# A float32 trunk of two macaron layers on one core: a plain first part of four feature tiles instead of five, and the low parts of the normalized features and of their sums computed by GpSimd instead of VectorE

## The chip, the cores and the metric

One core of one Trainium2 chip runs the whole program in one launch. The metric is the device time of one execution in microseconds (us), the median of three runs. Engines carry the names of the profile: PE is TensorE (PEld its weight loads), DVE is VectorE, ACT is ScalarE, POOL is GpSimd, SP is SyncE, which issues the weight transfers.

## What is computed

Input x is 512 positions by 1024 features, float32, one batch. Two layers run one after the other, each in three steps:

```python
def swiglu(h, w_gate, w_up, w_down):
    return (jax.nn.silu(h @ w_gate) * (h @ w_up)) @ w_down
...
        x = x + 0.5 * swiglu(rms_norm(x, ffn1_norm[l]), ffn1_w_gate[l], ffn1_w_up[l], ffn1_w_down[l])
        h = rms_norm(x, mix_norm[l])
...
        x = x + jnp.concatenate([conv_out, diff_out], axis=-1) @ w_out[l]
        x = x + 0.5 * swiglu(rms_norm(x, ffn2_norm[l]), ffn2_w_gate[l], ffn2_w_up[l], ffn2_w_down[l])
```

The gate and up matrices are 1024 by 2816, the down matrix 2816 by 1024. The middle step (a causal convolution group beside a differential attention group) is the same in both kernels and is called the mixer below. The change lies in the four SwiGLU blocks, called FFN 1 to 4 in the order in which they run.

## The kernel before

**Data and products.** x stays in SBUF with features on the partitions: eight tiles of 128 features by 512 positions. Each float32 number of a product is split in two: a high part rounded to the fp32r type (a copy on ACT) and a low part, the number minus its high part (a subtract, on DVE for most). A product is three fp32r matmuls that add up in PSUM: high by high, high by low, low by high. Lines 136 to 142 (`mm3`) issue these for matmuls of 512 columns, lines 374 to 380 (`product`) for those of 256. The normalized x of the plain part lacks its row factor r; its parts are `acth` and `actl`, and r is multiplied in as the result leaves PSUM (L710, L712).

**One FFN** (`ffn`, L682 to L752) works through the 22 feature tiles of 128 hidden features in the three parts of `PARTS` (L45).

*The plain part* takes the first five tiles. A tile is 48 matmuls of 512 columns for gate and up. Then come silu on ACT (L711), the product on DVE (L713), and the split of that product (`Gated.plain`: `hh` by ACT at L624, `hl` by DVE at L625). Once all tiles are through, the plain down products run, three matmuls per tile for each of the eight output tiles, with weights brought together by `gather` (L121) in chunks of eight 128-column blocks and split at L101 and L102. Each output tile's PSUM is added to x at L730.

*The two other parts* take eight and nine tiles with a scheme of seven half-size products in place of eight (a Winograd form of the 2 by 2 block product). A unit of class `GateUp` does one tile with 84 matmuls of 256 columns, a unit `Down` two of eight output tiles. Each unit needs sums of its weight blocks, made by POOL (L355 to L358), and four split operands named A, B, C and D (ACT at L364, DVE at L368). The units follow each other; a unit issues the parts of the next one at fixed places between its own products (`body`).

**The operands of the feature side** for these units are made in `Halves`, during the plain part. Eight times L310 forms hn, a tile of x times gain times r. For each of four steps j, DVE makes three sums of halves of two tiles (L314 to L317, four operations of 256 columns, `ht` with two slots that the steps take in turn), ACT takes their high parts (L318, `th`, 768 columns), and L319 their low parts (`tl`). Before the plain down products, `settle` overwrites `acth` and `actl` with the high and low parts of the eight hn themselves (L324 and L325): the gate and up products of the plain part, which read the old content, must have ended for that. Unit 0 of the first of the two parts reads `th`, `tl`, `acth` and `actl`.

**What sets the order.** The program is written as above, and a scheduler with a timeline of its own fixes the order of instructions on each engine when the kernel is built; `keep_in_program_order` pins some of them. On the chip each engine runs its queue strictly in that order and waits on semaphores. Rings of buffers bound how far loads run ahead: five raw weight blocks (`wraw`), four high parts, four low parts; a raw block comes free once its low part has been computed. In the first FFN only, `aside` (L687) puts some preparation of the attention bias into the loop over plain tiles.

Of the kernel before, what the change touches and what calls it, by code (L numbers as in the profile page):

```python
# [15 lines left out]
ALU = mybir.AluOpType  # L16
# [25 lines left out]
HS = SEQ // 2  # L42


PARTS = ((0, 5, 0), (5, 8, 3), (13, 9, 3))  # L45
PLAIN = PARTS[0][1]
PIN = False

# [20 lines left out]
def trunk(ctx: ExitStack, tc: tile.TileContext, xt, par, lamv, relb, onehot,  # L69
          gu1, dn1, wag, wqkv, wout, gu2, dn2, out):  # L70
    nc = tc.nc
    V, S, G, T = nc.vector, nc.scalar, nc.gpsimd, nc.tensor
# [9 lines left out]
    def f32(ap):  # L82
        return ap.bitcast(F32)
# [22 lines left out]
    def chunk(src, eng=None, pin=False):  # L106
        raw, hi, lo = ring("wraw"), ring("whi"), ring("wlo")
        nc.sync.dma_start(raw, src)
        parts_of(raw, hi, lo, eng, pin=pin)
        return hi, lo  # L110
# [36 lines left out]
    acth = act.tile([P, KT, SEQ], F32R, tag="acth", name="acth")  # L147
    actl = act.tile([P, KT, SEQ], F32R, tag="actl", name="actl")
# [17 lines left out]
    for k0, k1 in ((0, 1), (1, 4), (4, KT)):  # L166
        h = slice(k0 * P, k1 * P)
# [14 lines left out]
    def col(l, name, i=0):  # L182
        c = _AT[name] + i
        return pars[l][:, c : c + 1]
# [31 lines left out]
    class Prep:  # L216


        def __init__(self, l, gain):
            self.l, self.gain = l, gain  # L220
            self.hi, self.lo = acth, actl
            self.s = tmp.tile([P, SEQ], F32, tag="ssum", name="ssum", bufs=1)
# [35 lines left out]
    def lead_products(pr, w, ps):  # L258

        for k in range(KT):  # L260
            for n in range(2):
                for i in range(2):
                    mm3(ps[n][i], wpart(w[n][i], k), pr[k], k == 0, k == KT - 1)

        for k in range(KT):
            pr.squares(k, pin=True)

    def first_products(pr, w, ps, early=False):


        if not early:
            rc, v = rows_rstd(pr.s, DM)
            r = spread(rc, "rb")
        for k in range(KT):
            if early and k == STATS_AT:
                rc, v = rows_rstd(pr.s, DM, pin=True)
            for i in range(2):
                mm3(ps[0][i], wpart(w[0][i], k), pr[k], k == 0, k == KT - 1, pin=early and k in (0, STATS_AT))
        for i in range(2):
            for k in range(KT):  # L280
                if early and i == 0 and k == STATS_AT:
                    r = spread(rc, "rb", pin=True)
                mm3(ps[1][i], wpart(w[1][i], k), pr[k], k == 0, k == KT - 1, pin=early and k in (0, STATS_AT))
        return rc, v, r
# [4 lines left out]
    def pair_banks(turn):  # L289
        tag = turn_tag(turn)  # L290
        return [bank(tag, "ps_pair") for _ in range(2)]


    class Halves:
# [4 lines left out]
        def __init__(self, fp, pr, r):  # L299
            self.th = fp.tile([P, 3, KT // 2, HS], F32R, tag="th", name="th")  # L300
            self.tl = fp.tile([P, 3, KT // 2, HS], F32R, tag="tl", name="tl")

            self.whole = []
            free = [f"{t}{n}" for t in ("hh", "hl") for n in range(5, 9)]
            a, b = slice(0, HS), slice(HS, SEQ)
            ht = fp.tile([P, 2, 3, HS], F32, tag="ht", name="ht")
            for j in range(KT // 2):
                for k in (j, j + KT // 2):
                    h = fp.tile([P, SEQ], F32, tag=free.pop(), name="hn")
                    V.scalar_tensor_tensor(h, x[:, k, :], col(pr.l, pr.gain, k), r, op0=ALU.mult, op1=ALU.mult)  # L310
                    self.whole.append((k, h))
                (_, ha), (_, hb) = self.whole[-2:]
                t = ht[:, j % 2]
                V.tensor_tensor(t[:, 1], hb[:, b], ha[:, b], op=ALU.subtract)  # L314
                V.tensor_tensor(ha[:, b], ha[:, a], ha[:, b], op=ALU.subtract)
                V.scalar_tensor_tensor(t[:, 0], ha[:, b], -1.0, hb[:, b], op0=ALU.mult, op1=ALU.subtract)
                V.scalar_tensor_tensor(t[:, 2], t[:, 0], -1.0, hb[:, a], op0=ALU.mult, op1=ALU.subtract)  # L317
                S.activation(self.th[:, :, j, :], t, AF.Copy)  # L318
                V.tensor_tensor(self.tl[:, :, j, :], t, f32(self.th[:, :, j, :]), op=ALU.subtract)  # L319

        def settle(self):

            for k, h in self.whole:
                S.activation(acth[:, k, :], h, AF.Copy)  # L324
                V.tensor_tensor(actl[:, k, :], h, f32(acth[:, k, :]), op=ALU.subtract)  # L325

        def get(self, name):
            if name[0] == "t" and name != "t1":
# [353 lines left out]
    def ffn(pr, gu, dn, after, turn, lead=None, aside=None):  # L682
        with tc.tile_pool(name="ffn", bufs=1) as fp:
            r = halves = None
            held, h = [], Gated(fp, 0)
            for m in range(PLAIN):
                if m == 4 and aside:  # L687
                    aside()
                if lead and m < 2:
                    w = lead[m]  # L690
                else:
                    w = [(by_halves if lead and m == 2 else chunk)(gu[m, 0]), chunk(gu[m, 1])]
                held.append((m, w, pair_banks(turn + m)))
                if m == 0:
                    continue
                if m == 1 and lead:
                    lead_products(pr, [h[1] for h in held], [h[2] for h in held])
                    continue
                if m == 1:
                    _, _, r = first_products(pr, [h[1] for h in held], [h[2] for h in held])  # L700
                elif r is None:
                    rc = products(pr, w, held[-1][2][0], 0, 4, lambda: rows_rstd(pr.s, DM, pin=True)[0])
                    r = products(pr, w, held[-1][2][1], 1, 3, lambda: spread(rc, "rb", pin=True))
                else:
                    for i in range(2):
                        products(pr, w, held[-1][2][i], i)
                for n, _, ps in held:
                    gs = fp.tile([P, 2, SEQ], F32, tag="gn", name="gs", bufs=2)
                    us = gs[:, 1]
                    V.tensor_tensor(gs[:, 0], ps[0], r, op=ALU.mult)  # L710
                    S.activation(gs[:, 0], gs[:, 0], AF.Silu)  # L711
                    V.tensor_tensor(us, ps[1], r, op=ALU.mult)  # L712
                    V.tensor_tensor(us, us, gs[:, 0], op=ALU.mult)  # L713
                    h.plain(n, us)
                held = []
                if not halves:
                    halves = Halves(fp, pr, r)
            turn += PLAIN
            halves.settle()
            blocks = [divmod(kk, HALF) for kk in range(PLAIN)]  # L720
            blocks = [(half, m * HALF + f) for m in range(KT) for half, f in blocks]
            w = None
            for m in range(KT):
                ps = bank(turn_tag(turn + m // 2), "ps_d")
                for kk in range(PLAIN):
                    b = m * PLAIN + kk
                    if b % 8 == 0:
                        w = gather(dn, blocks[b : b + 8])
                    mm3(ps, wpart(w, b % 8), h.hh[kk], kk == 0, kk == PLAIN - 1)
                V.scalar_tensor_tensor(x[:, m, :], ps, 0.5, x[:, m, :], op0=ALU.mult, op1=ALU.add)  # L730
            turn += KT // 2

            units = []
            for m0, many, pairs in PARTS[1:]:
                h = Gated(fp, pairs)
                for n in range(many):
                    units.append(GateUp(fp, turn, halves, gu[m0 + n, 0], gu[m0 + n, 1], n, h))
                    turn += 1
                end = m0 + many == FT
                for q in range(KT // 2):  # L740
                    units.append(Down(fp, turn, dn, m0, many, pairs, q, h, after if end else lambda m: None,
                                      end and q == KT // 2 - 1))
                    turn += 1
            units[0].load()
            for k in "ABDC":
                units[0].hi(k, False)
                units[0].lo(k, False)
            for n, unit in enumerate(units):
                unit.body(units[n + 1] if n + 1 < len(units) else None, units[n - 1] if n else None,
                          units[n - 2] if n > 1 else None)  # L750
            units[-1].rest()
        return turn  # L752
# [371 lines left out]
    def aside():  # L1124
        make_scalars()
        make_bias()
# [92 lines left out]
```

## Time and profile before

| | |
|---|---|
| median of three runs | 1775.17 us (1774.72 to 1776.59) |
| the profiled execution | 1774.2 us, of which the span in the trace is 1772.4 us |
| granted clock of TensorE | 1.00 |
| first matmul of the units, FFN 1 to 4 | 89.9, 627.5, 970.2, 1507.9 us |

The profiled execution is one run, and all rows of a trace belong to it. A row of a timeline has the start and the duration in us, the engine, the line, the operation, out<-in with the shapes, the count (x3: three back to back), and in brackets the idle time before it with what ended that. Groups of a line have busy time in us, the mean duration in ns, and idle time. Matmuls are pipelined: a row's duration is longer than the distance to the next, and the distance of the starts is what one costs.

### The profile page before, as it was taken

The page shows a single profiled execution, that of the slowest core. Times are in us where ns is not written, and L with a number is a line of the kernel's source. Part 1 is how long each engine was busy: PE and PEld are TensorE (multiplying, and loading weights), DVE is VectorE, ACT ScalarE, POOL GpSimd, SP SyncE. Part 2 cuts the span into 40 slices and gives each one's busy share as a digit, 9 for nine tenths or more (in the row PEclk, how much of TensorE's full clock was granted, in tenths as well). Part 3 has the DMA queues.
Part 4 walks back from the last instruction along what each step waited for, and adds up shares of the span by engine and source line. Part 5 has one row for each costly group of instructions (what it writes and reads, how often), then busy time and mean ns, then how long its engine had stood idle before and what let it go on. Part 6 is the DMA issues. An engine that isn't in the chain of part 4 may idle for free.

```text
span 1772.4 us, 30241 instructions
## 1 busy us (share of the span) xinstructions
PE 1762.0 (99%) x11725; PEld 1617.0 (91%) x11725; DVE 1395.4 (79%) x1997; ACT 985.2 (56%) x1579; POOL 965.3 (54%) x665
## 2 busy tenths in 40 slices
PE   9999999999999999999999999999999999999999
PEld 7899999988788899999988999999887888999998
DVE  6978787868857878788767887877788588787875
ACT  6456465645845456466534664665558354564653
POOL 2276566379863156566304655653798533565661
PEclk9999999999999999999999999999999999999999
DMA  6232333422122233333332333334230232223332
GB/s 225 98 111 96 107 108 105 142 88 95 37 84 85 82 98 110 104 105 116 114 96 72 108 97 108 106 99 152 72 117 27 72 108 75 105 96 108 108 105 75
DMA packets 74225, 177.87 MB, mean 100 GB/s; under 512 B 8951, under 2 KB 30726, under 8 KB 74080
## 3 DMA queue, kind: packets, MB, share of 16 engines
q1 hardware_dynamic: 72480, 174.10, 29.6%
q8 instruction: 92, 1.51, 0.3%
q0 software_dynamic: 1312, 1.67, 0.3%
q14 instruction: 53, 0.43, 0.1%
q10 hardware_dynamic: 288, 0.16, 0.0%
HBM read 173.79 MB, written 3.42 MB: 100 GB/s over the span
## 4 chain that ended last, share of the span: by engine, by line
PE 89%; DVE 6%; issue 2%; POOL 2%; ACT 1%; DMA 0%; DVEq 0%; SPq 0%; ACTq 0%
PE ps_pair L378 48%; PE ps_pair L142 5%; PE ps_pair L141 5%; PE ps_pair L138 5%; PE ps_d L378 3%; DVE wlo L368 2%; PE ps_d L141 2%; PE ps_d L138 2%; PE ps_d L142 2%; PE ps_sc L990 2%; PE ps_pair L868 2%; PE ps_pair L867 2%; PE ps_pair L866 2%; PE ps_out L142 1%; PE ps_out L141 1%
## 5 line engine op out<-in xcount | busy, mean ns | idle before, releaser
L368 DVE TENSOR_TENSOR wlo<-wraw,whi 128x1024 fp32r<-128x1024 f32 (+4 forms) x400 | 507.0, 1269 | 171.4 <-ACT whi L364 170.5
L364 ACT ACTIVATE whi<-wraw 128x1024 fp32r<-128x1024 f32 (+4 forms) x400 | 373.5, 935 | 331.5 <-PE ps_pair L378 151.7
L355 POOL TENSOR_TENSOR wraw<-wraw 128x512 f32<-128x512 f32 (+1 forms) x100 | 127.8, 1278 | 554.7 <-DVE wlo L368 376.5
L378 PE MATMUL ps_pair<-actl,whi 128*128 128x256 f32 x1088 | 307.9, 283 | 0.0
L378 PE MATMUL ps_pair<-acth,wlo 128*128 128x256 f32 x1088 | 307.9, 283 | 0.0
L378 PE MATMUL ps_pair<-acth,whi 128*128 128x256 f32 x1088 | 307.9, 283 | 0.0
L378 PE MATMUL ps_pair<-th,whi 128*128 128x256 f32 x816 | 231.7, 284 | 0.9
L378 PE MATMUL ps_pair<-tl,whi 128*128 128x256 f32 x816 | 230.9, 283 | 0.0
L378 PE MATMUL ps_pair<-th,wlo 128*128 128x256 f32 x816 | 230.9, 283 | 0.0
L101 ACT ACTIVATE whi<-wraw 128x1024 fp32r<-128x1024 f32 (+3 forms) x124 | 123.4, 1001 | 155.4 <-PE ps_pair L141 83.1
L378 PEld LDWEIGHTS ps_pair<-acth,whi 128*128 128x128 f32 x1088 | 208.9, 192 | 0.2
L378 PEld LDWEIGHTS ps_pair<-actl,whi 128*128 128x128 f32 x1088 | 208.9, 192 | 0.2
L378 PEld LDWEIGHTS ps_pair<-acth,wlo 128*128 128x128 f32 x1088 | 208.9, 192 | 0.0
L141 PE MATMUL ps_pair<-actl,whi 128*128 128x512 f32 x448 | 174.5, 391 | 0.3
L142 PE MATMUL ps_pair<-acth,wlo 128*128 128x512 f32 x448 | 173.9, 390 | 0.0
L138 PE MATMUL ps_pair<-acth,whi 128*128 128x512 f32 x448 | 173.1, 392 | 0.2
L357 POOL TENSOR_TENSOR wraw<-wraw 128x512 f32<-128x512 f32 (+1 forms) x100 | 168.1, 1681 | 7.8
L358 POOL TENSOR_TENSOR wraw<-wraw 128x512 f32<-128x512 f32 (+1 forms) x100 | 163.6, 1636 | 7.8
L378 PEld LDWEIGHTS ps_pair<-th,whi 128*128 128x128 f32 x816 | 156.6, 192 | 2.5 <-ACT keep L427 2.5
L378 PEld LDWEIGHTS ps_pair<-tl,whi 128*128 128x128 f32 x816 | 156.6, 192 | 0.0
L378 PEld LDWEIGHTS ps_pair<-th,wlo 128*128 128x128 f32 x816 | 156.6, 192 | 0.0
L356 POOL TENSOR_TENSOR wraw<-wraw 128x512 f32<-128x512 f32 (+1 forms) x100 | 151.0, 1510 | 7.6
(203 smaller groups left out, 4404.7 us busy)
## 6 DMA issues: line engine op xcount, KB each, us to landing
wraw<-in_gu SPq DMA_DIRECT2D x172, 512.0 KB, 3.4
wraw<-in_wqkv SPq DMA_DIRECT2D x24, 512.0 KB, 3.5
wraw<-in_wag SPq DMA_DIRECT2D x16, 512.0 KB, 3.4
wraw<-in_wout SPq DMA_DIRECT2D x16, 512.0 KB, 3.5
wraw<-in_dn SPq DMA_DIRECT2D x60, 128.0 KB, 3.0
wraw<-in_dn SPq DMA_DIRECT2D x20, 384.0 KB, 3.1
wraw<-in_dn SPq DMA_DIRECT2D x28, 256.0 KB, 2.9
wraw<-in_dn SPq DMA_DIRECT2D x20, 320.0 KB, 3.4
```

What stands on the lines that cost most here:

```text
L101: S.activation(hi, raw, AF.Copy)
L138: first = T.matmul(ps, wh, xh, start=start, stop=False)
L141: T.matmul(ps, wh, xl, start=False, stop=False)
L142: T.matmul(ps, wl, xh, start=False, stop=stop)
L355: G.tensor_tensor(d, g1, u1, op=ALU.add)
L356: G.tensor_tensor(u1, u1, u2, op=ALU.add)
L357: G.tensor_tensor(m0, u1, g1, op=ALU.add)
L358: G.tensor_tensor(m1, m0, g2, op=ALU.add)
L364: pinned(S.activation(hi[:, : self.cols[k]], self.raw[k][:, : self.cols[k]], AF.Copy), pin)
L368: pinned(V.tensor_tensor(out=lo[:, :c], in0=self.raw[k][:, :c], in1=f32(hi[:, :c]), op=ALU.subtract), pin)
L378: mm = T.matmul(ps, l, r, start=first and i == n == 0, stop=False, skip_group_check=True)
L866: T.matmul(ps[n], xh[:, t], wh, start=k == 0, stop=False)
```

## The change

Five lines change. The plain part takes four tiles, the second part nine; the third stays. The low parts `tl` (four of 768 columns in each FFN) and `actl` (eight of 512 in each FFN) are subtracted by POOL. `aside` is called one tile earlier in the loop, at the last tile of four as before at the last of five.

```diff
-PARTS = ((0, 5, 0), (5, 8, 3), (13, 9, 3))
+PARTS = ((0, 4, 0), (4, 9, 3), (13, 9, 3))
...
                 S.activation(self.th[:, :, j, :], t, AF.Copy)
-                V.tensor_tensor(self.tl[:, :, j, :], t, f32(self.th[:, :, j, :]), op=ALU.subtract)
+                G.tensor_tensor(self.tl[:, :, j, :], t, f32(self.th[:, :, j, :]), op=ALU.subtract)
...
                 S.activation(acth[:, k, :], h, AF.Copy)
-                V.tensor_tensor(actl[:, k, :], h, f32(acth[:, k, :]), op=ALU.subtract)
+                G.tensor_tensor(actl[:, k, :], h, f32(acth[:, k, :]), op=ALU.subtract)
...
             for m in range(PLAIN):
-                if m == 4 and aside:
+                if m == 3 and aside:
                     aside()
```

The scheduler builds the order anew. In the built kernel the mixers and the third parts have the same orders as before on DVE, ACT, POOL and SP; the plain part and the second part of each FFN differ.

## The prediction

> **What bounds the kernel now.** I read the page's busy line, its chain of waits, then the timelines of PE, DVE and POOL around the second of the four FFN calls, which the change rebuilds.
>
> ```profile
> span 1772.4 us, 30241 instructions
> PE 1762.0 (99%) x11725; PEld 1617.0 (91%) x11725; DVE 1395.4 (79%) x1997; ACT 985.2 (56%) x1579; POOL 965.3 (54%) x665
> PE 89%; DVE 6%; issue 2%; POOL 2%; ACT 1%; DMA 0%; DVEq 0%; SPq 0%; ACTq 0%
> 90.02 25.81 PE ps_pair L378 x215
> ```
>
> PE works 99% of the span, so only two things move the time: the number of matmuls, and stops that are put into PE's stream. The last line is a piece of the chain: 215 matmuls of 256 columns in 25.81 us, 0.120 us each. Those of 512 columns follow each other at 0.227 us, as the end of the plain gate and up products of FFN 2 shows:
>
> ```profile
> 600.09 0.39 PE L142 MATMUL ps_pair<-acth,wlo 128*128 128x512 f32 x1
> 600.32 0.39 PE L138 MATMUL ps_d<-hh,whi 128*128 128x512 f32 x1
> ...
> 627.29 0.39 PE L142 MATMUL ps_d<-hh,wlo 128*128 128x512 f32 x1
> 627.52 0.28 PE L378 MATMUL ps_pair<-acth,whi 128*128 128x256 f32 x1
> ```
>
> The plain down products follow without a stop, and unit 0 follows them. The stage holds together because DVE is just in time: a row further down shows the last tile's low part (L625) at 609.86, ending at 610.55, and the down products that need it come after 48 others, at 600.32 + 48 x 0.227 = 611.2. The slack is 0.7 us. That is the place where the change acts.
>
> Whether DVE is in time depends on POOL. These are the rows of POOL and of DVE in the same stretch:
>
> ```profile
> 595.71 1.30 POOL L355 TENSOR_TENSOR wraw<-wraw 128x512 f32<-128x512 f32 x1 [35.71 <-DMA wraw<-in_gu]
> 597.09 2.17 POOL L356 TENSOR_TENSOR wraw<-wraw 128x512 f32<-128x512 f32 x1
> 599.34 1.63 POOL L357 TENSOR_TENSOR wraw<-wraw 128x512 f32<-128x512 f32 x1
> 601.04 1.63 POOL L358 TENSOR_TENSOR wraw<-wraw 128x512 f32<-128x512 f32 x1
> ```
>
> ```profile
> 575.91 1.21 DVE L102 TENSOR_TENSOR wlo<-wraw,whi 128x1024 fp32r<-128x1024 f32 x1
> 577.04 0.67 DVE L625 TENSOR_TENSOR hl<-gs,hh 128x512 fp32r<-128x512 f32 x1
> 577.64 0.41 DVE L315 TENSOR_TENSOR hn<-hn 128x256 f32<-128x256 f32 x1
> 577.98 0.41 DVE L316 SCALAR_TENSOR_TENSOR ht<-hn 128x256 f32<-128x256 f32 x1
> ...
> 594.46 0.95 DVE L319 TENSOR_TENSOR tl<-ht,th 128x768 fp32r<-128x768 f32 x1
> 595.33 0.68 DVE L710 TENSOR_TENSOR gs<-ps_pair,rb 128x512 f32<-128x512 f32 x1
> 595.94 2.15 DVE L102 TENSOR_TENSOR wlo<-wraw,whi 128x1024 fp32r<-128x1024 f32 x1
> 598.02 3.50 DVE L325 TENSOR_TENSOR actl<-hn,acth 128x512 fp32r<-128x512 f32 x2
> 601.44 1.78 DVE L368 TENSOR_TENSOR wlo<-wraw,whi 128x512 fp32r<-128x512 f32 x1
> ...
> 607.88 0.68 DVE L325 TENSOR_TENSOR actl<-hn,acth 128x512 fp32r<-128x512 f32 x1
> 608.49 0.68 DVE L713 TENSOR_TENSOR gs<-gs 128x512 f32<-128x512 f32 x1
> 609.86 0.69 DVE L625 TENSOR_TENSOR hl<-gs,hh 128x512 fp32r<-128x512 f32 x1 [0.70 <-ACT hh L624]
> ```
>
> Alone, a DVE subtract of 1024 columns takes 1.21 us, of 512 0.68, and they start 1.14 and 0.60 apart (0.34 for 256 columns). While POOL adds, the same L102 takes 2.15 and two L325 take 3.50. POOL's adds stretch too, from 1.30 to 2.17 and 1.63. So a DVE operation with two operands in SBUF and a POOL operation do not run side by side here: they take turns, one by one. From 595.94 to 603.22 DVE did work of 1.14 + 2 x 0.60 + 0.60 = 2.94 us and POOL the rest of L355 and three adds of 1.3, 4.97 us: 7.9 us of work in 7.28 us. I use that factor, 0.92, for work of both in one row.
>
> **The change part by part.** *Matmuls.* Per FFN the plain part loses one tile: 48 matmuls of gate and up and 24 of down, of 512 columns. The second part gains one unit, 84 of 256 columns, and its four Downs, now nine tiles wide, gain 6 of 512 each. Net: -48 x 0.227 + 84 x 0.120 = -10.9 + 10.1 = -0.8 us, four times: **-3.2 us**. This holds only while PE doesn't wait. The added unit brings what each unit of the third part brings already, whose nine units and nine-wide Downs run in before without a stop; I cost its sums, low parts and loads at nothing, hidden by its 84 matmuls (10.1 us).
>
> *DVE to POOL.* Per FFN eight low parts of 512 columns (L325) and four of 768 (L319) leave DVE:
>
> ```profile
> L325 DVE TENSOR_TENSOR actl<-hn,acth 128x512 fp32r<-128x512 f32 x32 | 29.1, 937 | 0.0
> L319 DVE TENSOR_TENSOR tl<-ht,th 128x768 fp32r<-128x768 f32 x16 | 14.9, 948 | 0.0
> L975 POOL TENSOR_TENSOR actl<-u,acth 128x512 fp32r<-128x512 f32 x6 | 6.6, 1094 | 1.7 <-ACT acth L974 1.7
> L102 POOL TENSOR_TENSOR wlo<-wraw,whi 128x1024 fp32r<-128x1024 f32 x44 | 105.4, 2401 | 31.6 <-ACT whi L101 31.6
> ```
>
> POOL's own rows for such a subtract are 1.094 us at 512 columns and 2.401 at 1024, so about 1.75 at 768 (my estimate between the two). DVE is freed of 8 x 0.60 + 4 x 0.87 = 8.3 us, POOL is given 8 x 1.09 + 4 x 1.75 = 15.7 us. On two engines that don't run side by side the stage's joint work grows by 7.4 us, while one tile fewer makes the stage 16 us shorter.
>
> *Order and waits.* The built order decides the rest. In FFN 2 and 4, POOL's queue is: sums L355 and L356 of unit 0, a low part L319, L357, L319, L358, then all eight L325 and the last two L319. The buffer ht has two slots, so L314 of the third and fourth step waits for POOL's first and second L319. On DVE, behind these waiting L314, stand both steps (eight operations of 256 columns), the weights' L102, and last the low part L625 of the last plain tile. PE meets that low part after 39 down matmuls, 8.9 us after the end of gate and up; that end, M, is 600.3 - 10.9 = 589.4.
>
> When does L625 come? The slot for unit 0's second block is freed by the L102 at 575.91 to 577.1; the landing takes 3.4 us, so the sums start at 580.5, where in before they started at 595.71.
>
> ```profile
> wraw<-in_gu SPq DMA_DIRECT2D x172, 512.0 KB, 3.4
> ```
>
> From there POOL has four sums (1.15 us each without the wait: the long L355 below ended 1.15 after DVE let go), three L319 and eight L325 ahead of or between DVE's work: 4.6 + 5.25 + 8.7 = 18.6 us. DVE has three L102 (3.4), the rest of the first two steps (1.0), the D low part (0.6), two L713 and two L625 (2.4) and the two steps (2.7): 10.1 us; L710 and L712 read PSUM and run beside POOL. Together 28.7 x 0.92 = 26.4, and 0.7 for the wait on ACT's high part: 580.5 + 27.1 = 607.6, that is M + 18.2 against M + 8.9. **PE stops for some 9.4 us in FFN 2, and the same in FFN 4**, whose queues are alike.
>
> In FFN 1 and 3 the two steps stand behind the last L625, so the delay is smaller. FFN 1, M = 62.66 - 10.9 = 51.8:
>
> ```profile
> 62.66 0.39 PE L138 MATMUL ps_d<-hh,whi 128*128 128x512 f32 x1
> ```
>
> ```profile
> 59.43 0.68 DVE L625 TENSOR_TENSOR hl<-gs,hh 128x512 fp32r<-128x512 f32 x1
> 60.63 0.68 DVE L625 TENSOR_TENSOR hl<-gs,hh 128x512 fp32r<-128x512 f32 x1
> ```
>
> ```profile
> 64.29 1.72 POOL L355 TENSOR_TENSOR wraw<-wraw 128x512 f32<-128x512 f32 x1 [19.07 <-DMA wraw<-in_gu]
> ```
>
> Before, these low parts of tiles 2 and 3 came at M + 8.3 and M + 9.5 with POOL silent until 64.29. Now three or four of POOL's operations (1.09 each) fall between, 3.8 us: M + 12.1, against M + 9.5 (42 matmuls of cover). That is 2.6 us, and unit 0's first low part behind the two steps adds an estimated 2.2: **5 us** (bounds 0 and 8). In FFN 3 ten DVE operations (6.6 us) and eight of POOL (8.8) stand between M and the last low part: 15.4 x 0.92 = 14.1 against M + 9.5: **4.6**, say 5.
>
> Sum: 5 + 9.4 + 5 + 9.4 - 3.2 = **+25.6 us**. The profiled run was 1774.2 us (its span 1772.4 and 1.8 around it), so 1799.8; the median of the runs is 1.0 above the profiled one: **1801**.
>
> The bound on this is the opposite habit of the port, seen once:
>
> ```profile
> 940.30 5.33 POOL L355 TENSOR_TENSOR wraw<-wraw 128x512 f32<-128x512 f32 x1 [34.79 <-issue]
> ```
>
> ```profile
> 940.05 0.42 DVE L316 SCALAR_TENSOR_TENSOR ht<-hn 128x256 f32<-128x256 f32 x1
> ...
> 944.06 0.42 DVE L317 SCALAR_TENSOR_TENSOR ht<-ht,hn 128x256 f32<-128x256 f32 x1
> ```
>
> One POOL add took 5.33 us while DVE ran nine short operations back to back. If DVE always held on so, L625 of FFN 2 would wait only for the sums and L319 that L314 needs: 3 x 1.15 + 2 x 1.75 + 10.1 + 0.7 = 17.8 after 580.5, M + 8.9, no stop. So each long stop lies between 0 and 12 us (without the factor 0.92). I take the turns, since the rows from 595.94 on have the mix of lengths that the new stage has. The Trainium skill, in SBUF — State Buffer, section "Who interferes with whom", calls this an exclusive lock that whoever issues first holds for a whole instruction, and says: "Issue order, not op shape, decides who blocks." The rows at 598.02 agree with it; the long L355, passed over eight times, shows that issuing first is not all, and by that reading the sum would be -3.2 us.
>
> A long stop may also cool PE's clock. At the start nine matmuls of 512 columns took 3.67 us, 0.41 apart, though the granted clock reads 1.00 there:
>
> ```profile
> 1.04 3.67 PE L162 MATMUL ps_idle<-ones_r 128*128 128x512 f32 x9 [1.04 <-DVE relb L759]
> ```
>
> Paid once after each of two stops, that is up to 2 x 9 x 0.18 = 3.3 us. No row shows it after a stop within the run, so I take nothing and keep 3.3 as the upper end. The Trainium skill's TensorE: Matmul & The Clock Gate, Part 1, halves the clock after an idle window of about 3.4 us; by it the forecast would be 1804.
>
> **The rivals.** *A, DVE holds the port*, as at 940: stops of 0 to 3 us in some FFNs, where PE waits for the last L319 or L325 that POOL has then put off. 1775.2 - 3.2 + 0 to 7: 1772 to 1779, about 1775. For it: the row at 940.30; against it: every pair from 595.94 on. *B, all is hidden and DVE's relief also removes small stops*: 1772.0 or less. Against it: before has no stop in the FFNs to remove, and -3.2 us is 0.18% of the time, below what can be told from no change, which I put at 0.2% or 3.6 us. *C, slower still:* POOL is late into unit 1, whose sums come behind the last L319, so that the low parts of unit 1 are late as well; decisive once POOL's queue ends over 10 us (one unit) after unit 0 starts. Price: one more stop of 4 to 6 us in FFN 2 and 4, 1811 to 1818. A ends on the other side of the forecast: not slower. *That the change does nothing* would be 1775; the matmul counts exclude it as a cause, but A has the same time.
>
> **How the numbers follow.** Forecast 0.74, with a range of its own of 1785 to 1812: long stops from 5 to 11 us, short ones from 2 to 7, clock 0 to 3.3. A 0.16, of which 0.03 is slower by over 0.2%. B 0.04. C 0.06. The range, 1775 to 1812, leaves out B, the lower half of A and most of C, 0.17. Faster by over 0.2%: B, 0.04. Within: A, 0.13. Slower: 0.74 + 0.06 + 0.03 = 0.83.
>
> **What would show it.** In the profile after: a gap in PE's stream within the plain down products, before an L141 that takes the last tile's low part, some 9 us in FFN 2 and 4, 2 to 5 in FFN 1 and 3; DVE's 256-column operations and L713 there stretched to over 1 us beside POOL's L325, whose mean lies well over 1.094; and 48 fewer 512-column and 84 more 256-column matmuls per FFN net. If PE has no gap over 2 us, the turns were the wrong assumption. If the gaps stand before L378, the wait is for unit 0's parts, and the place was wrong. If DVE's operations are short but late, it is a wait in the order and not the port.

## The result, and the profile after

| | before | changed |
|---|---|---|
| median of four runs each | 1775.88 us (1774.72 to 1777.10) | 1823.31 us (1822.64 to 1823.51) |
| ratio | | 1.0269 (95% interval 1.0257 to 1.0281) |
| span of the profiled run | 1772.4 us | 1821.2 us, 48.8 longer |
| granted clock of TensorE, mean | 1.000 | 0.987 |

The direction was right, the size was not: 47 us slower where 25 were forecast, and outside the range. These are the lines of the changed kernel's page that answer to those shown of before:

```profile
span 1821.2 us, 30626 instructions
PE 1774.0 (97%) x11869; PEld 1630.0 (89%) x11869; DVE 1415.4 (78%) x1957; ACT 997.0 (55%) x1595; POOL 1074.0 (59%) x729
PEclk9899999999999899999999999999999998999999
PE 80%; DVE 12%; issue 2%; POOL 2%; DMA 2%; ACT 1%; DVEq 0%; SPq 0%; ACTq 0%; POOLq 0%
```

PE has gone from 99% to 97% busy, DVE's part of the chain has doubled, and the granted clock, 1.00 all through before, has three dips. DVE's busy time has risen by 20 us although 48 low parts left it. The added units brought some of that, but the 64 operations of L314 to L317, the same in both kernels, alone went from 26.0 to 56.9 us.

Where the time went can be read from the first matmul of the units in each FFN (90.63, 641.22, 990.72 and 1541.13 us, against 89.86, 627.52, 970.17 and 1507.85). With the matmul counts alone FFN 1's would come 72 x 0.227 = 16.3 us earlier, and each further stretch would be 0.8 us shorter. What is over is the loss: **17.1 us in FFN 1, 13.7, 7.7 and 13.5 in FFN 2 to 4**, 52.0 in all, less 3.2 for the matmuls: 48.8. After the last of these four marks the rest of the program takes 280.1 us, 15.5 more than before, just the added unit and the wider Downs: they cost what was reckoned.

The stops in PE's stream, from its timeline (in brackets the idle time and what ended it):

```profile
82.98 0.80 PE L138 MATMUL ps_d<-hh,whi 128*128 128x512 f32 x1 [12.03 <-DVE x L730]
...
621.82 1.65 PE L138 MATMUL ps_d<-hh,whi 128*128 128x512 f32 x3 [6.22 <-ACT hh L624]
626.46 0.79 PE L141 MATMUL ps_d<-hl,whi 128*128 128x512 f32 x1 [2.99 <-DVE hl L625]
...
973.21 0.50 PE L141 MATMUL ps_d<-hl,whi 128*128 128x512 f32 x1 [2.91 <-DVE hl L625]
975.44 0.80 PE L141 MATMUL ps_d<-hl,whi 128*128 128x512 f32 x1 [1.26 <-DVE hl L625]
...
1520.67 1.65 PE L138 MATMUL ps_d<-hh,whi 128*128 128x512 f32 x3 [6.21 <-ACT hh L624]
1525.31 0.80 PE L141 MATMUL ps_d<-hl,whi 128*128 128x512 f32 x1 [2.99 <-DVE hl L625]
```

In FFN 2 to 4 they stand where they were forecast, at the last tile's parts. In FFN 1 the stop is longer and at another place: PE waits for L730, which empties a PSUM bank.

DVE in FFN 2, in the same stretch:

```profile
606.03 1.51 DVE L314 TENSOR_TENSOR ht<-hn 128x256 f32<-128x256 f32 x1
607.47 2.86 DVE L102 TENSOR_TENSOR wlo<-wraw,whi 128x1024 fp32r<-128x1024 f32 x1
610.25 1.50 DVE L315 TENSOR_TENSOR hn<-hn 128x256 f32<-128x256 f32 x1
...
617.40 0.68 DVE L712 TENSOR_TENSOR gs<-ps_pair,rb 128x512 f32<-128x512 f32 x1
...
618.82 2.28 DVE L713 TENSOR_TENSOR gs<-gs 128x512 f32<-128x512 f32 x1
...
624.66 1.74 DVE L625 TENSOR_TENSOR hl<-gs,hh 128x512 fp32r<-128x512 f32 x1
```

Operations that take 0.42 us alone take 1.4 to 1.5 here, the subtract of 512 columns 1.74 instead of 0.68; L712, which reads PSUM, keeps its 0.68. That is the taking of turns, without a break from 606 to 626. POOL's low parts stretch as well, to means of 1.64 and 2.13 us.

The clock, from windows of the changed kernel (span, busy times by engine, then PEclk, DMA share, GB/s):

```profile
82.90:87.00 4.10, 4.02 (x10) 3.15 (x11) 4.10 (x6) 2.74 (x4) 2.50 (x3) 0.50 0.00 0
87.00:91.00 4.00, 4.00 (x20) 3.31 (x19) 4.00 (x4) 0.26 (x1) 3.34 (x2) 0.95 0.19 39
626.00:630.00 4.00, 3.54 (x8) 2.81 (x9) 2.37 (x4) 1.06 (x1) 3.59 (x3) 0.50 0.30 114
630.00:634.00 4.00, 4.00 (x19) 3.26 (x18) 4.00 (x4) 1.58 (x2) 2.69 (x3) 0.99 0.00 0
975.40:982.00 6.60, 6.56 (x16) 5.18 (x17) 6.46 (x6) 1.48 (x2) 5.58 (x4) 0.53 0.00 0
```

For about 4 us after a stop the granted clock is 0.50, and 10 matmuls are issued where 4 us otherwise hold 20. In the timeline they follow at 0.427 us instead of 0.227. Summed over the matmuls on record this costs 2.2, 2.4, 3.1 and 3.4 us in FFN 1 to 4, **11 us** in all.

A fifth such stretch lies in the mixer between FFN 1 and 2, which has the same order in both kernels. In both, PE pauses there for a gap of 1.1 us between two starts. In the changed kernel the clock is at 0.50 right after it, in before it stays at 1.00 (a window of the changed kernel, then one of before):

```profile
510.60:514.00 3.40, 3.40 (x18) 3.30 (x17) 2.39 (x11) 2.78 (x12) 2.91 (x3) 0.50 0.02 5
494.30:497.70 3.40, 3.40 (x24) 3.06 (x23) 3.32 (x14) 3.40 (x14) 2.93 (x3) 1.00 0.00 0
```

The same matmuls take 5.69 us there (510.24 to 515.93) and 4.13 in before (493.96 to 498.09): **1.6 us** more, which the marks above count under FFN 2.

### The profile page after: what moved, and what is told of

Its sections match the earlier page's. It is cut to its first block, busy times and chain, and to the rows that moved or that the text cites. A ratio compares the mean times of both kernels' runs of the same rounds, so it can differ in the third digit from the quotient of the medians.

```text
span 1821.2 us, 30626 instructions
## 1 busy us (share of the span) xinstructions
PE 1774.0 (97%) x11869; PEld 1630.0 (89%) x11869; DVE 1415.4 (78%) x1957; ACT 997.0 (55%) x1595; POOL 1074.0 (59%) x729
## 4 chain that ended last, share of the span: by engine, by line
PE 80%; DVE 12%; issue 2%; POOL 2%; DMA 2%; ACT 1%; DVEq 0%; SPq 0%; ACTq 0%; POOLq 0%
PE ps_pair L378 51%; PE ps_d L378 4%; PE ps_pair L141 2%; PE ps_pair L138 2%; PE ps_pair L142 2%; DVE wlo L368 2%; DVE wlo L102 2%; PE ps_sc L990 2%; PE ps_pair L868 2%; PE ps_pair L867 2%; PE ps_pair L866 2%; PE ps_out L138 1%; PE ps_out L141 1%; PE ps_out L142 1%; PE ps_d L141 1%
## 5 line engine op out<-in xcount | busy, mean ns | idle before, releaser
L368 DVE TENSOR_TENSOR wlo<-wraw,whi 128x1024 fp32r<-128x1024 f32 (+2 forms) x416 | 534.2, 1285 | 186.7 <-ACT whi L364 185.9
L364 ACT ACTIVATE whi<-wraw 128x1024 fp32r<-128x1024 f32 (+2 forms) x416 | 391.4, 944 | 369.6 <-PE ps_pair L378 157.3
L355 POOL TENSOR_TENSOR wraw<-wraw 128x512 f32<-128x512 f32 (+1 forms) x104 | 129.7, 1247 | 485.9 <-DVE wlo L368 390.3
L378 PE MATMUL ps_pair<-acth,wlo 128*128 128x256 f32 x1152 | 326.0, 283 | 0.0
L378 PE MATMUL ps_pair<-actl,whi 128*128 128x256 f32 x1152 | 326.0, 283 | 0.0
L378 PE MATMUL ps_pair<-acth,whi 128*128 128x256 f32 x1152 | 326.0, 283 | 0.0
L378 PE MATMUL ps_pair<-th,whi 128*128 128x256 f32 x864 | 245.3, 284 | 1.2 <-ACT keep L427 0.5
L378 PE MATMUL ps_pair<-tl,whi 128*128 128x256 f32 x864 | 244.5, 283 | 0.0
L378 PE MATMUL ps_pair<-th,wlo 128*128 128x256 f32 x864 | 244.4, 283 | 0.0
L378 PEld LDWEIGHTS ps_pair<-acth,whi 128*128 128x128 f32 x1152 | 221.2, 192 | 0.2
L378 PEld LDWEIGHTS ps_pair<-actl,whi 128*128 128x128 f32 x1152 | 221.2, 192 | 0.2
L378 PEld LDWEIGHTS ps_pair<-acth,wlo 128*128 128x128 f32 x1152 | 221.2, 192 | 0.0
L358 POOL TENSOR_TENSOR wraw<-wraw 128x512 f32<-128x512 f32 (+1 forms) x104 | 176.4, 1696 | 7.9
L357 POOL TENSOR_TENSOR wraw<-wraw 128x512 f32<-128x512 f32 (+1 forms) x104 | 170.2, 1637 | 14.4 <-DVE wlo L368 3.7
L378 PEld LDWEIGHTS ps_pair<-th,whi 128*128 128x128 f32 x864 | 165.8, 192 | 2.9 <-ACT keep L427 2.9
L378 PEld LDWEIGHTS ps_pair<-th,wlo 128*128 128x128 f32 x864 | 165.8, 192 | 0.0
L378 PEld LDWEIGHTS ps_pair<-tl,whi 128*128 128x128 f32 x864 | 165.8, 192 | 0.0
L356 POOL TENSOR_TENSOR wraw<-wraw 128x512 f32<-128x512 f32 (+1 forms) x104 | 157.5, 1515 | 7.7
L141 PE MATMUL ps_pair<-actl,whi 128*128 128x512 f32 x384 | 149.5, 391 | 0.3 <-DVE actl L227 0.2
L138 PE MATMUL ps_pair<-acth,whi 128*128 128x512 f32 x384 | 148.4, 393 | 1.3 <-DVE gs L710 0.7
L142 PE MATMUL ps_pair<-acth,wlo 128*128 128x512 f32 x384 | 149.0, 391 | 0.0
```

The lines of the kernel that those rows point to most:

```text
L138: first = T.matmul(ps, wh, xh, start=start, stop=False)
L141: T.matmul(ps, wh, xl, start=False, stop=False)
L142: T.matmul(ps, wl, xh, start=False, stop=stop)
L355: G.tensor_tensor(d, g1, u1, op=ALU.add)
L356: G.tensor_tensor(u1, u1, u2, op=ALU.add)
L357: G.tensor_tensor(m0, u1, g1, op=ALU.add)
```

## The experiments

The theory, T: DVE and POOL take turns, so DVE's last operations of the plain part come late and PE, which needs them in order, stops. Rivals: R1, four tiles cover too little, whoever computes the low parts; R2, the wait of L314 for POOL's tl is the harm; R3, POOL's queue is simply long and is waited for in line, with no port in it. Ratios are to runs of before on the same chip, whose medians lay at 1775.0 to 1775.9 us.

**The parts of the change alone**: e1 undoes both low parts, e2 the tiles, e3 the low parts of 512 columns, e4 those of 768.

```diff
 e1: both lines back to V.tensor_tensor, PARTS as changed
 e2: PARTS = ((0, 5, 0), (5, 8, 3), (13, 9, 3)), both lines with G.tensor_tensor
 e3: tl by G, actl by V      e4: tl by V, actl by G      (both with PARTS as changed)
```

> Four plain tiles, all low parts back on DVE. Theory T (DVE and POOL take turns, and what PE waits for stands in line behind it): with POOL left to unit 0's four sums the last tile's low part comes about 2 us late in FFN 2 and 4 and hardly late in FFN 1 and 3; four stops of 0 to 3 us and a cold clock of 0 to 2 us after some: 1774 to 1790 us. Rival R1 (the smaller cover of four tiles, 39 to 42 down products instead of 48, makes the stops, whoever computes the low parts): 1805 us or more, stops of 5 us and over in every FFN.

> Five plain tiles as before, the low parts on POOL. T: the joint work of DVE and POOL grows by 7.4 us per FFN with only 0.7 us of slack; some of it falls under the fifth tile's gate and up, so stops of 2 to 7 us each with 2 us of cold clock behind the longer ones: 1785 to 1810 us. R1: no stops, 1772 to 1779 us.

> Four plain tiles, only the four low parts of 768 columns (tl) on POOL, those of 512 on DVE. T: POOL's share is 7.0 of 15.7 us, DVE still waits for it at L314, but no eight L325 stand ahead of the last tl; about half of the loss: 1785 to 1805 us. Rival R2 (the wait of L314 for POOL's tl is all the harm, turns at the port cost nothing): near the changed kernel, 1812 to 1825 us.

> Four plain tiles, only the eight low parts of 512 columns (actl) on POOL, tl on DVE, so that no DVE instruction of the plain part waits for POOL. T: DVE's last low part is still delayed by turns with POOL, by some 5 us in FFN 2 and 4 and less in the others, 1780 to 1800 us. R2: as with all low parts on DVE, that is within 3 us of e1_parts_only.

| | median | ratio (95% interval) | loss in FFN 1 to 4 by the units' first matmul |
|---|---|---|---|
| e1, four tiles | 1792.15 us | 1.0095 (1.0078 to 1.0112) | 6.7, 6.3, 4.2, 3.5 |
| e2, low parts by POOL | 1782.86 us | 1.0042 (1.0027 to 1.0057) | 7.5, 0.0, 0.0, 0.1 |
| e3, four tiles, tl by POOL | 1800.75 us | 1.0142 (1.0126 to 1.0157) | 8.2, 10.8, 5.8, 6.3 |
| e4, four tiles, actl by POOL | 1811.12 us | 1.0201 (1.0186 to 1.0217) | 15.6, 9.7, 6.4, 10.1 |

(The losses are those of the profiled run. A stop inside unit 0 counts in the next FFN's column, and so does a half clock in the mixer between, some 1.6 us in FFN 2 of e3 and in FFN 4 of e1, e3 and e4.) e1 missed upward, e4 too: both parts alone cost something, 17 and 8 us, and together 47. e3 came as expected. R1 has a share: with four tiles PE stops even with every low part on DVE, most in FFN 1. It isn't all, since e1 lies 31 us under the changed kernel. Nor is that share simply DVE having too much to do. In FFN 2 to 4 the longest stops of e1 are waits for L730, and DVE was idle for 1.85 us shortly before that, at the D part of unit 1: POOL's sum for it was late, having taken 3.5 to 3.7 us instead of 1.29 while DVE ran on. These are PE, DVE and POOL of e1 in FFN 2:

```profile
617.79 0.50 PE L138 MATMUL ps_d<-hh,whi 128*128 128x512 f32 x1 [1.66 <-DVE x L730]
```

```profile
615.92 1.21 DVE L368 TENSOR_TENSOR wlo<-wraw,whi 128x512 fp32r<-128x512 f32 x1 [1.85 <-ACT whi L364]
```

```profile
611.58 3.64 POOL L355 TENSOR_TENSOR wraw<-wraw 128x512 f32<-128x512 f32 x1 [11.64 <-DMA wraw<-in_gu]
```

e2 is under what T gave: with five tiles the same low parts on POOL cost nothing in FFN 2 to 4, as the fifth tile's gate and up, 10.9 us of PE, cover the turns. Its whole loss is one stop in FFN 1 and the clock behind it:

```profile
77.24 0.80 PE L141 MATMUL ps_d<-hl,whi 128*128 128x512 f32 x1 [4.35 <-DVE hl L625]
```

So the two edits spend the same slack. R2 falls as the whole of it: e4, in which DVE waits for no tl of POOL, is 19 us slower than e1. My note that nothing on DVE waits for POOL in e4 was wrong, though, as FFN 1 shows. POOL and DVE there:

```profile
60.09 12.58 POOL L325 TENSOR_TENSOR actl<-hn,acth 128x512 fp32r<-128x512 f32 x6
72.63 1.26 POOL L355 TENSOR_TENSOR wraw<-wraw 128x512 f32<-128x512 f32 x1
```

```profile
74.59 1.20 DVE L368 TENSOR_TENSOR wlo<-wraw,whi 128x512 fp32r<-128x512 f32 x1 [9.27 <-ACT whi L364]
```

DVE stands idle for 9.27 us: L368, the D part of unit 1, needs POOL's sum L355, and this stands in POOL's queue behind six L325. The L730 that PE waits for stand behind L368.

**No reading by POOL**: the low parts replaced by fills of the operand that POOL had read (tl and actl aren't computed), two in e6, three in e10. `tl` is also filled with zeros once in each FFN.

```diff
+            G.memset(f32(self.tl), 0.0); free = [f"{t}{n}" for t in ("hh", "hl") for n in range(5, 9)]
...
-                G.tensor_tensor(self.tl[:, :, j, :], t, f32(self.th[:, :, j, :]), op=ALU.subtract)
+                for _ in range(2): G.memset(t, 0.0)
...
-                G.tensor_tensor(actl[:, k, :], h, f32(acth[:, k, :]), op=ALU.subtract)
+                for _ in range(2): G.memset(h, 0.0)
```

> The changed kernel with each of POOL's twelve low parts per FFN replaced by two fills of the operand that it had read (so the low parts tl and actl are left out of the computation); POOL's queue, its waits and DVE's waits for it stay, but POOL reads nothing from SBUF in them. T: the turns go, so DVE runs at its own pace: in FFN 2 and 4 the two stops (6.6 and 3.6 us) shrink to 0 to 3 us in all, in FFN 3 to 0 to 1, and in FFN 1 only the part that POOL's queue makes by being served in order remains, 3 to 8 of 12.4 us: 1780 to 1795 us. Rival R3 (no port: POOL's instructions are long and DVE waits for them in line): the stops stay within a third of the changed kernel's, 1810 us or more.

> As e6_memset with three fills in place of two (tl and actl are left out of the computation), so that POOL's queue in the stage is at least as long as with the low parts: 3 x 0.528 and 3 x 0.741 us against 1.29 and 1.81 us for the subtracts alone. T (the turns make DVE late): the stops of FFN 2 to 4 stay at 0 to 3 us each, FFN 1 has 3 to 8 us: 1778 to 1792 us. R3 (the length of POOL's queue, whatever it does): stops as in the changed kernel, 1808 us or more; half-way, 1792 to 1808, would give both a share.

Measured: e6 1777.70 us, 1.0011 (1.0002 to 1.0021), below what T gave; e10 1784.36 us, 1.0048 (1.0030 to 1.0066), within it. The losses by FFN are 4.3, 0.8, 0.0, 0.0 in e6, and in e10 2.3, 7.4, 0.0, 0.0 where 5.3 us of the 7.4 are a stop in FFN 1's unit 0. Groups of e10 on POOL, and on DVE:

```profile
L325 POOL MEMSET hn<- 128x512 f32 x96 | 47.5, 524 | 3.4 <-DVE ht L317 1.6 <-DVE ht L316 1.5
L319 POOL MEMSET ht<- 128x768 f32 x48 | 35.0, 740 | 0.4 <-ACT th L318 0.4
```

```profile
L713 DVE TENSOR_TENSOR gs<-gs 128x512 f32<-128x512 f32 x16 | 10.8, 682 | 0.1
L315 DVE TENSOR_TENSOR hn<-hn 128x256 f32<-128x256 f32 x16 | 6.6, 418 | 0.2
```

POOL works 82.5 us on the fills, where the changed kernel's low parts took 85.8 with all their waiting; yet DVE's operations beside them are back at 682 and 418 ns (976 and 1028 in the changed kernel), and FFN 2 to 4 have no stop.

The built orders are not all the same, though. In FFN 2 and 4 the changed kernel has all eight operations of the last two steps ahead of the last low part, e6 has seven and e10 only four. FFN 3 is free of this: there DVE has the same order up to the last low parts in all three kernels, and in the changed kernel and e10 POOL is busy beside it without a break. From the start of the L713 shown to the end of the two L625 DVE takes 10.2 us in the changed kernel (first pair of lines) and 5.3 in e10 (second pair):

```profile
965.21 1.78 DVE L713 TENSOR_TENSOR gs<-gs 128x512 f32<-128x512 f32 x1
971.41 3.97 DVE L625 TENSOR_TENSOR hl<-gs,hh 128x512 fp32r<-128x512 f32 x2
```

```profile
942.09 0.68 DVE L713 TENSOR_TENSOR gs<-gs 128x512 f32<-128x512 f32 x1
946.10 1.28 DVE L625 TENSOR_TENSOR hl<-gs,hh 128x512 fp32r<-128x512 f32 x2
```

R3 falls for FFN 3. For FFN 2 and 4 little is left of it: had the other four operations stood ahead of e10's last low part, with the wait of 1.26 us for POOL's fill that they show, it would have come 3.0 us later and some 0.6 us too late (an estimate from these rows), where the changed kernel stops for 9.8. The fills write tl's and actl's place not at all or early, so waits of unit 0 for POOL are not reproduced, but the stops in question stand before unit 0. The Trainium skill (SBUF — State Buffer, "Who interferes with whom") says that a two-input DVE instruction contends with a GpSimd instruction that reads SBUF, not with one that only writes it; these runs agree.

**FFN 1**: e7 gives the sums of halves four slots, so that L314 never waits for POOL; e11 also has DVE make the first sum of FFN 1's unit 1.

```diff
 e7:  steps j = 2, 3 write buffers of their own (tags s0 to s2) in place of ht[:, j % 2]
 e11: as e7, and in FFN 1 for units[1]
-            G.tensor_tensor(d, g1, u1, op=ALU.add)
+            V.tensor_tensor(d, g1, u1, op=ALU.add)
```

> The changed kernel with four slots for the sums of halves instead of two (steps 3 and 4 in buffers of their own, their high and low parts in two pieces each), so that no L314 waits for POOL. T: the stop of FFN 1, which stood behind that wait, falls from 12.4 to under 5 us; in FFN 2 to 4 the turns remain, 4 to 9 us of stops each: 1795 to 1812 us. If the wait for the slot were all of it: 1785 us or less.

> As e7_more_slots, and in FFN 1 the first sum of unit 1 by DVE, so that DVE's D low part of unit 1 no longer waits for a sum that stands behind eight low parts in POOL's queue. If that wait is what stops PE in FFN 1 of e7 (7.1 us) and nothing else is late: the stop goes, 1797 to 1802 us. If POOL is simply too long there: the stop in the down products goes but one of 4 to 8 us comes before or inside unit 0, which needs tl: 1803 to 1810 us.

Measured: e7 1807.53 us, 1.0185 (1.0161 to 1.0210); e11 1805.10 us, 1.0163 (1.0147 to 1.0179). e7's time lies where T put it, but FFN 1's stop fell only to 7.1 us: DVE now stands 10.48 us idle at the D part of unit 1. POOL and DVE of e7 (its L335 is the low part L325, L365 the sum L355, L378 the low part L368):

```profile
61.26 14.15 POOL L335 TENSOR_TENSOR actl<-hn,acth 128x512 fp32r<-128x512 f32 x8
75.37 1.26 POOL L365 TENSOR_TENSOR wraw<-wraw 128x512 f32<-128x512 f32 x1
```

```profile
77.33 1.07 DVE L378 TENSOR_TENSOR wlo<-wraw,whi 128x512 fp32r<-128x512 f32 x1 [10.48 <-ACT whi L374]
```

So the wait that R2 names has a share, since e7 lies some 15 us under the changed kernel, but its order is new in other places too. In e11 the wait for L355 is gone and PE reaches unit 0 at 80.68 us instead of 87.32, but there it stops three times for POOL's tl. That is mostly the second outcome that was written down: POOL is late in FFN 1 in both, at different places. One stop of 3.0 us is left in the down products of e11 (before 68.28), at a low part that stands on DVE behind the moved sum, which waits for its transfer. The three stops in unit 0:

```profile
83.91 0.39 PE L388 MATMUL ps_pair<-tl,whi 128*128 128x256 f32 x1 [1.51 <-POOL tl L329]
85.68 0.39 PE L388 MATMUL ps_pair<-tl,whi 128*128 128x256 f32 x1 [1.15 <-POOL tl L329]
87.60 0.58 PE L388 MATMUL ps_pair<-tl,whi 128*128 128x256 f32 x1 [1.30 <-POOL tl L329]
```

**DVE's order with four tiles**: e9 is e1 with the last plain tile's low part and the eight low parts of 512 columns kept in this order. It also moves steps 3 and 4 into `settle` and pins their first operation (not shown).

```diff
-                V.tensor_tensor(actl[:, k, :], h, f32(acth[:, k, :]), op=ALU.subtract)
+                tc.keep_in_program_order(V.tensor_tensor(actl[:, k, :], h, f32(acth[:, k, :]), op=ALU.subtract))
```

> Four plain tiles, all low parts on DVE, with the eight low parts of 512 columns held behind the last plain tile's low part. If DVE's order is what is left of the loss in the kernel with the parts alone (1792 us), the stops in the plain down products of FFN 2 to 4 go and 1 to 4 us of waiting for actl may appear before unit 0: 1778 to 1790 us. If DVE has simply too much work for the shorter stage, the stops only move to unit 0: 1788 to 1800 us.

Measured: 1795.07 us, 1.0105 (1.0088 to 1.0122), no better than e1. In FFN 1 PE now stops inside unit 0 (4.96 us between two starts), for a weight's low part that stands behind the moved operations. In FFN 2 to 4 the expectation had the place wrong: the longest stops of e1 were waits for L730 already, and in e9 they still are, now with the eight moved low parts ahead of it. Neither order lets DVE serve PE in time; that no order could isn't shown.

## Why the prediction was wrong

| term | forecast | measured |
|---|---|---|
| matmuls | -3.2 us | -3.2 us |
| stops in FFN 2, 3, 4 | 9.4, 5, 9.4 us | 9.8, 4.5, 9.8 us |
| stops in FFN 1 | 5 us | 14.5 us |
| cold clock in the FFNs | 0 (upper end 3.3) | 11 us |
| cold clock in a mixer | 0 | 1.6 us |
| sum | 25.6 us | 48.0 us of the 48.8 |

The measured stops are the distances of two starts less the usual one; the 0.8 us left over I can't place, some matmul records being missing.

- **What bounds, and the matmul count**: right to 0.1 us.
- **The turns, and the late low part in FFN 2 to 4**: right in place and size. The landing was put at 580.5 and the low part's end 27 us later; measured from L355's start at 598.98 to 626.40 it took 27.4. It came as two stops, for the high part and for the low part of the last tile. The size owes something to luck: POOL's subtracts were priced at 1.09 and 1.75 us, while with DVE idle (FFN 1, from 66.56 on) they took 1.29 and 1.81, and the joint work ran faster than the factor 0.92 by about as much. That the turns are the cause is shown by e10 in FFN 3, with the same order on DVE, and by its DVE durations everywhere; for FFN 2 and 4 it rests on the estimate above.
- **FFN 1**: this step failed. I followed the low parts L625 and unit 0's first low part, but not the L730 that free PSUM banks. Neither of the two waits that made up my 5 us came: PE passes both places without a stop. It stops 12.2 us for L730 instead. On DVE these stand behind both steps, these behind POOL's first tl, and that in POOL's queue behind six L325. The changed kernel's POOL and DVE:

```profile
60.09 10.26 POOL L325 TENSOR_TENSOR actl<-hn,acth 128x512 fp32r<-128x512 f32 x6
70.31 1.81 POOL L319 TENSOR_TENSOR tl<-ht,th 128x768 fp32r<-128x768 f32 x1
```

```profile
72.15 1.47 DVE L314 TENSOR_TENSOR ht<-hn 128x256 f32<-128x256 f32 x1 [6.69 <-POOL tl L319]
73.65 1.91 DVE L315 TENSOR_TENSOR hn<-hn 128x256 f32<-128x256 f32 x1
...
82.24 2.48 DVE L730 SCALAR_TENSOR_TENSOR x<-ps_d,x 128x512 f32<-128x512 f32 x4
```

  DVE idles for 6.69 us and then needs from 72.15 to 82.24, again in turns, for nine operations that take 3.3 us alone (eight of 0.34 us and one of 0.60, by the distances of starts before). Three small stops of 0.7 to 0.9 us earlier in FFN 1 were not in the sum either.
- **The clock**: this step failed too. It was taken as nothing, with 3.3 us as its upper end for two stops, because no row showed it after a stop. The first matmuls of the program, at 0.41 us, were the right row; the 1.00 beside them was no reading, since the clock record of that trace begins only at 3.96 us. It was paid in all four FFNs, and once in a mixer. The Trainium skill's rule (TensorE: Matmul & The Clock Gate, Part 1) was the better guide, and the granted clock of 0.50 for 4 us agrees with it; the stretch in the mixer, after a gap of only 1.1 us, does not fit its idle window of about 3.4 us.
- **The rivals**: A, the port held by DVE, did not come about over the stage as a whole. B and the price of C were off as well: POOL was not late into unit 1.

## What to carry to other kernels

When work moves between two engines that take turns, add up the work of both for the stretch that PE's cover has to hide; what is freed on one is not freed, and two edits that each fit into the slack may not fit together. Follow every operation behind a waiting one in an in-order queue, those that free PSUM banks too, not only those that make operands. Give the half clock behind the stops of PE a term of its own: here it cost 2.2 to 3.4 us in each FFN.

## What was not expected of the hardware

Who gets the port seems to hang on less than a tenth of a microsecond. In FFN 2, e7 and e11 have the same queues on DVE and POOL, and in both POOL's first sum started while DVE was in an operation that reads PSUM. In e7 it started 0.09 us before DVE's next operation; POOL went ahead, and the turns lasted to the end of the stage. In e11 it started 0.04 us before the same operation, and DVE ran seven operations back to back before POOL's got through (POOL and DVE of e7, then of e11):

```profile
594.36 1.29 POOL L365 TENSOR_TENSOR wraw<-wraw 128x512 f32<-128x512 f32 x1 [21.34 <-DMA wraw<-in_gu]
594.45 1.48 DVE L325 SCALAR_TENSOR_TENSOR ht<-hn 128x256 f32<-128x256 f32 x1
```

```profile
595.33 4.67 POOL L365 TENSOR_TENSOR wraw<-wraw 128x512 f32<-128x512 f32 x1 [21.40 <-DMA wraw<-in_gu]
595.37 0.41 DVE L325 SCALAR_TENSOR_TENSOR ht<-hn 128x256 f32<-128x256 f32 x1
```

The stop of PE at the last low part was 7.3 us (distance of two starts) in the one and 1.1 in the other, which then has one of 2.2 us before unit 0. The runs of e7 spread from 1804.97 to 1814.45 us, with the profiled one the longest; that this choice makes the spread isn't shown. What decides stays open, two cases being all there is; that DVE keeps the port as long as its operations follow without a gap fits all the long POOL rows shown, but was only argued.

The clock also went cold after stops of 2.7 us (e3, before 85.47) and not after one of 3.2 (e1, before 963.84). After the gap of 1.1 us it did so in one or both mixers of some kernels (the changed one, e1, e3, e4) and in neither of others (before, e2, e6, e10). So a stop's length alone doesn't tell.

No version tried beats the kernel before. e6 says why: even with POOL's low parts free of the port, and not computed at all, the four-tile kernel stays at 1777.7 us, because FFN 1 alone loses 4.3 us (in its profiled run of 1776.15), more than the 3.2 that the matmuls save.
